# A two-layer attention trunk on one core: new tables of priorities and engine choices for a scheduler that writes the instruction order

## The chip, the cores and the metric

One Trainium2 chip, one of its cores. The metric is the device time of one execution in microseconds (us). A time is a median of several runs; the profile is of one execution.

## The reference

Two layers run over 256 tokens of width 1024. In each, the normalised input `h` goes through one large projection (1024 x 9808); its columns feed three causal attentions of 8 heads, each with a SiLU gate, a projection of its own and a sigmoid merge gate. One more projection adds the result to the residual.

```python
def hybrid_layer(x, gain, w_in, f_bias, w_branch, w_out):
    h = rms_norm(x, gain)
    proj = jnp.einsum('bsd,de->bse', h, w_in)
    (qa, ka, va, ga, qb, kb_, vb_, gb, qc, kc, vc, gc,
     q_idx, k_idx, w_idx, f_logit, merge_logit) = jnp.split(proj, SPLIT_POINTS, axis=-1)
    oa = moba_attention(rope(qa), rope(ka), va) * silu(ga)
    ob = dsa_attention(rope(qb), rope(kb_), vb_, qi, ki, wi) * silu(gb)   # keys chosen by an indexer, top 64
    oc = forgetting_attention(qc, kc, vc, log_f) * silu(gc)
    y = jnp.einsum('nbsw,nwd->bsnd', jnp.stack([oa, ob, oc]), w_branch)
    merged = jnp.sum(sigmoid(merge_logit).reshape(B, S, 3, D_MODEL) * y, axis=2)
    return x + jnp.einsum('bsd,de->bse', merged, w_out)
```

After the two layers stands a last `rms_norm`. All is float32.

## The kernel before

**Matrix products.** Each float32 matrix is split into a high part that TensorE takes in one pass (`wh`, `hTh`, `og0h`) and the remainder (`wl`, `hTl`, `og0l`). A product is three matmuls: high by high, high by remainder, remainder by high. ScalarE (ACT) writes the high part (L444 for weights), VectorE (DVE) the remainder (L448). A weight piece is 128 x 1024 elements; it comes by DMA into one of four `raw` buffers and its parts go into rings of six `wh` and six `wl`.

**Units.** The work is cut into units of one block of outputs each: `unit_b` (128 columns of the input projection by 256 tokens, 24 matmuls), `unit_a` (values and output projection, 512 columns), `unit_m` (merge gates, `mth`), `unit_y` (branch outputs, with L1017 and L1019 merging them). All matmuls of projections are recorded at L486; they write one of three PSUM banks `proj`, and an element-wise instruction must have read a bank before it is used again.

**Attention.** For two heads at a time, `Pair.attend` computes scores, exponentials (L779), the normalised probabilities in two float16 halves (`p hi` at L787 on ScalarE or L790 on VectorE, `p lo` at L794), transposes them by DMA (`t<-e`, L803) and copies the result to float32 (`pt<-t`, L808 on ScalarE or L809 on VectorE). The matmuls L821 to L824 multiply with the values. L837 to L842 apply the gate; GpSimd (POOL) does a few of these products (`og`) and of the merges (`y`).

**Order.** Every operation is an object with a number, a priority `key` (the number of the unit that it belongs to, with an offset) and one or more `ways`: engine, cost in ns, and the function that emits it. Numbers are given in program order and do not depend on the tables below. `Plan.run` is a list scheduler that runs while the program is built: it keeps a clock for each engine from fixed costs, takes the engine that can start first, and among the operations of that engine that could start within a slack of the earliest it emits the one with the lowest key. The slack is 0 for TensorE, 110 ns for ScalarE and VectorE, and 1500 ns for SyncE (SP), which issues nearly all DMAs. What it emits is each engine's static program; at run time the engines wait only for semaphores, each in its own order.

Two tables correct the scheduler:

```python
        o.key += SHIFT.get(o.n, 0.0)
        if len(ways) > 1 and o.n in WAY:
            o.ways = [w + (WAY[o.n],) if w[0] == "DVE" else w for w in ways]
```

A negative `SHIFT` brings an operation forward. A way's extra numbers are added to its end time when ways are compared, so that `WAY` of -1500 forces an operation to VectorE and +1500 forces it away. VectorE's way of a `p hi` or a `pt` copy carries 500 ns (`AWAY`) against it anyway. The scheduler reckons 1250 ns for the issue of a transpose (`T_ISSUE`) and 1500 ns until it has landed (`T_LAND`), always the same, and has no instruction fetches.

The operations that are spoken of by number:

- 0, 1: loads of the first 128 rows of `x`; 3, 4: of the second 128 rows; 71, 80, 89, 98, 116, 125: the weight chunks va0, va1, va2, va3, va5, va6 (256 KB each) that the first units use. Before the shifts, the keys of va0 to va7 are -95 + 0.2 i, those of 3 and 4 -94.7 and -94.69.
- 17, 18, 19: pieces of the first norm; 46: half of the squares of the second 128 rows; 126: the high part of va6.
- 637, 692, 1059, 1391, 2241, 2463: `pt` copies; 548, 909, 2193, 2458: `p hi`, all ten on ScalarE before.
- 2673, 2680: weight loads of `vb` in layer 1; 2754: of `kb`; 3127: the third of the four `w_branch` loads for the last branch of layer 1. Their loads, the transposes and the loads of `w_out` all go through SyncE's queue.
- 3100: matmuls of a unit of that last branch; 3175, 3177, 3212: of the output projection.

Of the kernel before, what the change touches and what calls it, by code (L numbers as in the profile page):

```python
# [63 lines left out]
def constants(forget_bias):  # L64
# [24 lines left out]


SHIFT = {
# [31 lines left out]
}  # L123
WAY = {
# [6 lines left out]
}  # L131


# [1169 lines left out]
```

## Time and profile before

| | us |
|---|---|
| median of 3 runs | 602.27 (600.35 to 602.92) |
| the profiled execution | 601.2 |
| its span, first to last instruction | 599.4 |

The span is what the profile's parts are shares of; 1.8 us of the execution lie around it. A row of a group names line, engine, operation, output and inputs, shapes, count, then busy time and the mean of one in ns. Rows of waits give the waiting instruction, what ended the wait, the total in us, how many, and the longest. Rows of stretches give the bounds, then each engine's busy time and instructions in the order TensorE, its weight loads (PEld), VectorE, ScalarE, GpSimd, then granted clock, DMA share and GB/s. Rows of the timeline and of the chain start with the start and the duration in us. Matmuls overlap: a busy time of 0.28 us of a 128 x 256 matmul is not the distance to the next one.

### The profile page before, as it was taken

The numbers are of one execution on the slowest core, as the hardware profiler recorded it, in microseconds if no ns is written. First come the engines' busy times: TensorE is split into PE (matmuls) and PEld (weight loads), VectorE is DVE, ScalarE is ACT, GpSimd is POOL, SyncE is SP. The second block draws the span as 40 slices with busy tenths as digits, with TensorE's granted clock in tenths as the row PEclk, the third lists the DMA queues.
The fourth block names the chain that finished last, engine by engine and source line by source line (L and its number), as shares of the span: only waits on it lengthen the run. The fifth ranks groups of instructions, "written<-read, shape, count | busy, mean of one in ns | idle before, by whom it ended". The sixth has DMA issues, their size and how long they took to land.

```text
span 599.4 us, 12672 instructions
## 1 busy us (share of the span) xinstructions
PE 587.5 (98%) x4704; PEld 567.8 (95%) x4704; DVE 542.3 (90%) x1360; ACT 463.8 (77%) x1004; POOL 92.4 (15%) x102
## 2 busy tenths in 40 slices
PE   9999999999999999999999999999999999999995
PEld 7999999999998999999889999999999899999885
DVE  8889999989999989999686999999998999999773
ACT  5769669987997879985485874999889787999632
POOL 1042133000000225110000421320000023340000
PEclk9999999999999999999999999999999999999999
DMA  8986286597865866397648447669869486645802
GB/s 314 305 282 210 73 233 182 162 226 213 241 182 140 271 195 164 89 286 245 189 150 262 152 143 235 178 186 208 214 188 256 121 246 208 169 133 129 311 35 72
DMA packets 136510, 116.83 MB, mean 195 GB/s; under 512 B 42752, under 2 KB 127360, under 8 KB 136448
## 3 DMA queue, kind: packets, MB, share of 16 engines
q1 hardware_dynamic: 136160, 115.59, 66.4%
q8 instruction: 37, 0.61, 0.4%
q10 hardware_dynamic: 288, 0.43, 0.2%
q14 instruction: 25, 0.20, 0.1%
HBM read 103.42 MB, written 1.05 MB: 174 GB/s over the span
## 4 chain that ended last, share of the span: by engine, by line
PE 58%; DVE 22%; ACT 9%; DMA 5%; issue 4%; POOL 0%; SPq 0%; POOLq 0%; DVEq 0%; ACTq 0%
PE proj L486 47%; DVE wl L448 7%; PE proj L1173 4%; DMA t<-e 4%; ACT wh L444 2%; PE proj L1113 2%; DVE isc L970 2%; DVE e L794 1%; DVE rsh L535 1%; ACT pt L808 1%; ACT e L779 1%; DVE t L969 1%; DVE isc L949 1%; DMA raw<-in_w_out_dram 1%; DVE rr L537 1%
## 5 line engine op out<-in xcount | busy, mean ns | idle before, releaser
L486 PE MATMUL proj<-hTh,wh 128*128 128x256 f32 x1024 | 265.7, 278 | 1.5 <-ACT mth L986 1.0
L486 PE MATMUL proj<-hTl,wh 128*128 128x256 f32 x1024 | 265.0, 277 | 0.0
L448 DVE TENSOR_TENSOR wl<-raw,wh 128x1024 fp32r<-128x1024 f32 x180 | 223.3, 1249 | 15.2 <-ACT wh L444 14.0
L486 PE MATMUL proj<-hTh,wl 128*128 128x256 f32 x1024 | 227.9, 276 | 0.0
L444 ACT ACTIVATE wh<-raw 128x1024 fp32r<-128x1024 f32 x180 | 188.7, 1054 | 38.6 <-PE proj L486 26.3
L486 PEld LDWEIGHTS proj<-hTh,wh 128*128 128x128 f32 x1024 | 192.2, 188 | 2.3 <-ACT mth L986 1.2
L486 PEld LDWEIGHTS proj<-hTl,wh 128*128 128x128 f32 x1024 | 192.2, 188 | 0.0
L486 PEld LDWEIGHTS proj<-hTh,wl 128*128 128x128 f32 x1024 | 172.9, 188 | 0.0
L536 POOL TENSOR_TENSOR rsh<-rsh,cst 128x256 f32<-128x256 f32 x40 | 32.4, 812 | 351.4 <-DVE rsh L535 323.2
L538 POOL TENSOR_TENSOR rr<-rr,rsh 128x256 f32<-128x256 f32 x40 | 45.6, 1140 | 2.8
L779 ACT ACTIVATE e<-e,st 128x128 f32<-128x128 f32 (+1 forms) x96 | 42.6, 445 | 2.9 <-DVE st L775 2.4
L794 DVE SCALAR_TENSOR_TENSOR e<-e,st 128x128 f16<-128x128 f32 (+1 forms) x96 | 40.1, 424 | 1.1 <-ACT e L787 0.4
L808 ACT ACTIVATE pt<-t 128x384 fp32r<-128x384 f16 x73 | 34.3, 513 | 7.1 <-DMA t<-e 6.8
L486 PE MATMUL proj<-wh,v 128*128 128x512 f32 (+1 forms) x144 | 35.2, 366 | 0.0
L486 PE MATMUL proj<-og0l,wh 128*128 128x256 f32 x128 | 33.8, 277 | 0.0
L486 PE MATMUL proj<-og0h,wh 128*128 128x256 f32 x128 | 32.4, 278 | 1.3 <-DVE mth L1017 1.3
L787 ACT ACTIVATE e<-e,st 128x256 f16<-128x256 f32 (+1 forms) x77 | 31.6, 445 | 2.7 <-DVE st L783 2.3
L486 PEld LDWEIGHTS proj<-wh,v 128*128 128x128 f32 x144 | 25.3, 189 | 4.3
L486 PE MATMUL proj<-og0h,wl 128*128 128x256 f32 x128 | 28.6, 276 | 0.0
L486 PEld LDWEIGHTS proj<-og0h,wh 128*128 128x128 f32 x128 | 24.0, 188 | 1.6 <-DVE mth L1017 1.5
L486 PEld LDWEIGHTS proj<-og0l,wh 128*128 128x128 f32 x128 | 24.0, 188 | 0.0
L486 PEld LDWEIGHTS proj<-og0h,wl 128*128 128x128 f32 x128 | 21.7, 188 | 0.0
(227 smaller groups left out, 1071.0 us busy)
## 6 DMA issues: line engine op xcount, KB each, us to landing
raw<-in_w_in_dram SPq DMA_DIRECT2D x74, 1024.0 KB, 5.5
raw<-in_w_branch_dram SPq DMA_DIRECT2D x24, 512.0 KB, 4.2
raw<-in_w_out_dram SPq DMA_DIRECT2D x8, 1024.0 KB, 8.4
raw<-in_x_dram SPq DMA_DIRECT2D x8, 256.0 KB, 4.9
tmp<-wf SPq DMA_DIRECT2D x16, 128.0 KB, 5.5
t<-e SPq DMA_TRANSPOSE x48, 2.9
raw<-in_w_in_dram SPq DMA_DIRECT2D x2, 320.0 KB, 6.2
x<-in_x_dram SPq DMA_DIRECT2D x2, 256.0 KB, 3.8
```

The costliest lines, as they stand in the source:

```text
L444: ACT.activation(p[0].v, sel(c.v), AF.Copy)
L448: DVE.tensor_tensor(p[1].v, sel(c.v), p[0].v.bitcast(F32), op=ALU.subtract)
L486: PE.matmul(o(), a(), b(), start=first and i == 0, stop=last and i == n - 1)
L536: gps(lambda: POOL.tensor_tensor(T(sh)[:np_], T(sh)[:np_], s[:np_], op=ALU.mult), S, [k_rope], [sh], key, "rope")
L538: gps(lambda: POOL.tensor_tensor(T(r)[:np_], T(r)[:np_], T(sh)[:np_], op=ALU.add), S, [sh], [r], key, "rope")
L779: act(lambda t=t, a=a, n=n, st=st, h=h: ACT.activation(ex(h, a, n), ex(h, a, n), AF.Exp, bias=T(st)[:, t:t + 1], scale=-1.0, accum_out=T(s ...
L787: ACT.activation(hi(a, n), ex(h, a, n), AF.Copy, scale=T(st)[:, 4 + t:5 + t])
L794: dve(lambda t=t, a=a, n=n, st=st, h=h, hi=hi, lo=lo: DVE.scalar_tensor_tensor(lo(a, n), ex(h, a, n), T(st)[:, 4 + t:5 + t], hi(a, n), op0 ...
L808: plan.op([("ACT", t_act(384, False), lambda to=to, src=src: ACT.activation(to(), src(), AF.Copy)), ("DVE", t_dve2(384), lambda to=to, src ...
L970: dve(lambda o=o, t8=t8: DVE.match_replace(o, T(t8), o, TAKEN), n, [t8], [k_isc[i]], key + r * step, "top8")
L1113: PE.matmul(T(ps[t]), h(i, t), v(w, n), start=left[t] == 23, stop=left[t] == 0)
L1173: PE.matmul(T(ps[t])[:, :w], hA[hi](a + x, t), T(p[wi])[:, ats[w > 256][wi]][:, :n * w].rearrange("p (k c) -> p k c", k=n)[:, x], start=le ...
```

## The change

Only the two tables are replaced: `SHIFT` has 315 entries instead of 327, `WAY` 47 instead of 53. 134 numbers have a shift in both (27 of them the same), 193 lose theirs, 181 get one. In `WAY`, 28 entries forced to VectorE and 25 away from it; now 31 and 16. The new values come from a replay of the order outside the kernel that also counts the fetches of instructions by DMA; `Plan.run` itself, its costs and all operations are the same.

```diff
 SHIFT = {
-    0: -11.5, 1: -7, 3: -11.5, 4: -11, 17: 2, 28: -8, 31: -6, 47: -11, 73: 4, 80: -12, 89: -2.5, 90: -11.5, 91: 1.5,
-    98: -8, 99: -9.5, 100: 2.5, 188: 3, 308: -7, 310: -7, 364: 6, 380: 2.5, 386: -12, 387: -7, 419: 3.5, 440: -11,
...
-    2672: 2.5, 2675: -12, 2678: -12, 2680: -4.5, 2688: -6.5, 2697: -12, 2701: -8.5, 2755: -12, 2774: -12, 2780: -3,
...
-    2940: -9.5, 2941: -12, 2942: -12, 2943: -12, 2945: 3.5, 2962: -12, 2964: -8.5, 2969: -9, 2989: -4, 2991: -11,
-    2992: -3, 3009: -4, 3044: -12, 3046: -9, 3048: -8, 3076: -12, 3079: -11.5, 3127: -7, 3175: -12, 3177: 6, 3212: 5,
+    0: -12, 1: -7.5, 3: -12, 4: -10.5, 18: -2.5, 19: -7.5, 22: -4.5, 28: -12, 31: -5.5, 38: -8, 46: -12, 47: -12,
+    55: -12, 71: -11.5, 80: -3.5, 89: -8.5, 90: -3.5, 91: 2, 98: -12, 100: 5, 116: -5.5, 117: -11.5, 125: -4.5,
+    126: -3, 174: -9, 186: -12, 187: 2, 188: 2.5, 218: -8.5, 219: -8, 220: -12, 221: -2.5, 228: 4, 243: -5, 263: 6,
...
+    2641: -11.5, 2652: -7.5, 2653: 6, 2669: -12, 2670: -12, 2673: -7, 2678: -12, 2680: -12, 2754: -12, 2780: -2,
...
+    2962: -11.5, 2973: -3.5, 2980: -12, 2985: -6, 2986: 5.5, 3005: -6, 3009: -9.5, 3018: -12, 3044: -6.5, 3046: -12,
+    3048: -12, 3050: -9.5, 3076: -12, 3100: -12,
 }
 WAY = {
-    17: -1500, 18: -1500, 90: -1500, 99: 1500, 489: 1500, 490: 1500, 539: 1500, 552: -1500, 553: -1500, 559: 1500,
-    631: 1500, 632: -1500, 650: -1500, 675: 1500, 687: -1500, 845: -1500, 862: -1500, 863: -1500, 914: -1500,
-    915: -1500, 996: 1500, 1215: 1500, 1240: 1500, 1283: -1500, 1290: 1500, 1373: -1500, 1391: 1500, 1392: -1500,
-    1416: 1500, 1417: -1500, 1443: 1500, 1489: 1500, 2115: -1500, 2194: 1500, 2207: -1500, 2211: -1500, 2212: -1500,
-    2249: -1500, 2255: 1500, 2411: -1500, 2558: -1500, 2571: -1500, 2603: -1500, 2661: 1500, 2790: 1500, 2791: 1500,
-    2802: 1500, 2827: 1500, 2841: 1500, 2846: -1500, 2852: 1500, 2940: 1500, 3009: -1500,
+    18: 1500, 19: -1500, 46: 1500, 90: -1500, 126: -1500, 509: 1500, 534: -1500, 547: 1500, 548: -1500, 631: 1500,
+    637: -1500, 692: -1500, 845: -1500, 862: -1500, 863: -1500, 909: -1500, 915: -1500, 1059: -1500, 1216: -1500,
+    1283: -1500, 1290: 1500, 1349: -1500, 1373: -1500, 1379: 1500, 1391: -1500, 1392: -1500, 1417: -1500, 1443: 1500,
+    1489: 1500, 2115: -1500, 2193: -1500, 2207: -1500, 2241: -1500, 2249: -1500, 2254: 1500, 2255: 1500, 2458: -1500,
+    2459: -1500, 2463: -1500, 2558: -1500, 2790: 1500, 2827: 1500, 2841: 1500, 2846: -1500, 2852: 1500, 3005: 1500,
+    3009: -1500,
 }
```

50 rows, old and new, of the table SHIFT are left out of this document.

## Prediction

> **What bounds the kernel now.** First the page's busy shares and queue rows, then the stretches, to see whether TensorE is bound by its own work.
>
> ```profile
> span 599.4 us, 12672 instructions
> PE 587.5 (98%) x4704; PEld 567.8 (95%) x4704; DVE 542.3 (90%) x1360; ACT 463.8 (77%) x1004; POOL 92.4 (15%) x102
> PEclk9999999999999999999999999999999999999999
> q8 instruction: 37, 0.61, 0.4%
> q14 instruction: 25, 0.20, 0.1%
> 135.00:150.00 15.00, 15.00 (x133) 14.95 (x132) 14.83 (x29) 11.65 (x20) 0.00 (x0) 1.00 0.70 213
> 105.00:120.00 15.00, 13.98 (x122) 13.68 (x121) 13.91 (x46) 14.76 (x41) 0.00 (x0) 1.00 0.56 160
> ```
>
> TensorE (PE) is busy for 98% of the span at nearly full granted clock. In the full stretch, 135 to 150, it starts 133 matmuls, one per 113 ns; in the stretch from 105 to 120 only 122. Eleven missing matmuls are 1.2 us. A new order changes no matmul, so it can win only such holes. The waits of TensorE list them (two rows of the first 7 us, before the projections begin, are left out).
>
> ```profile
> PE proj L486 <- DVE mth L1017: 1.3, 1, 1.3
> PE o L821 <- ACT pt L808: 1.1, 3, 0.5
> PE proj L486 <- ACT mth L986: 1.0, 1, 1.0
> PE proj L486 <- DVE g L736: 0.3, 2, 0.2
> PE proj L486 <- DVE rr L537: 0.3, 1, 0.3
> ```
>
> These are 4.0 us in 8 waits. A wait costs more than its idle time, because a busy matmul overlaps the next one. The timeline of TensorE at one of them shows how much:
>
> ```profile
> 100.07 0.28 PE L821 MATMUL o<-pt,v 128*128 128x256 f32 x1
> 100.19 0.22 PE L822 MATMUL o<-pt,v 128*128 128x128 f32 x1
> 100.30 0.28 PE L824 MATMUL o<-pt,v 128*64 128x256 f32 x1
> 101.02 0.39 PE L821 MATMUL o<-pt,v 128*128 128x256 f32 x1 [0.44 <-ACT pt L808]
> 101.25 0.22 PE L822 MATMUL o<-pt,v 128*128 128x128 f32 x1
> ```
>
> Undisturbed, the next start comes 0.12 us after a 128x256 matmul (100.07 to 100.19). Across the wait it is 0.72 (100.30 to 101.02): 0.60 lost for 0.44 idle, 0.16 more. The restarted matmul then holds its successor 0.23 instead of 0.12, another 0.11. So each wait costs its idle time plus 0.27, and all eight cost 4.0 + 8 x 0.27 = 6.2 us. That is the most a new order can win; everything below is a share of it.
>
> Which of them hang on a DMA is told by the chain of work and by two more rows of the timeline:
>
> ```profile
> 93.39 4.31 DMA t<-e
> 127.87 5.77 DMA t<-e
> 415.90 6.45 DMA t<-e
> 471.23 4.81 DMA t<-e
> 553.30 7.85 DMA raw<-in_w_out_dram
> DMA to landing us min/median/max: 2.7/2.9/6.7
> 479.53 0.50 PE L486 MATMUL proj<-wh,hTh 128*128 128x512 f32 x1 [0.16 <-DVE g L736]
> 563.87 0.39 PE L486 MATMUL proj<-og0h,wh 128*128 128x256 f32 x1 [1.34 <-DVE mth L1017]
> ```
>
> A transpose of the probabilities (`t<-e`, L803) lands 2.9 us after its issue in the median; the kernel's own scheduler reckons 1.25 + 1.5 = 2.75. The four in the chain took 4.3 to 6.5. Each stands ahead of a hole: 101.02 follows the first; the other two waits for `pt` follow the second and third; the one at 479.53 follows the fourth, through ScalarE and `g`. In an in-order queue a `pt` copy that waits for a late transpose holds everything behind it. These four holes cost 1.1 + 3 x 0.27 = 1.9, and 0.16 + 0.27 = 0.4: together 2.3 us. The wait at 563.87 costs 1.34 + 0.27 = 1.6; it stands behind the load of `w_out`, as VectorE shows:
>
> ```profile
> 559.00 0.42 DVE L477 SCALAR_TENSOR_TENSOR og0l<-ot,og0h 128x256 fp32r<-128x256 f32 x1
> 562.26 1.23 DVE L448 TENSOR_TENSOR wl<-raw,wh 128x1024 fp32r<-128x1024 f32 x1 [2.84 <-ACT wh L444]
> 563.40 0.75 DVE L1017 SCALAR_TENSOR_TENSOR mth<-mth,proj 128x256 f32<-128x256 f32 x2
> ```
>
> VectorE sat 2.84 us before a weight split whose data were late; the release of a `proj` bank (L1017) was queued behind it. The remaining waits (`mth` L986, `rr` L537, the other `g`: 1.0 + 0.3 + 0.2 idle, three waits) cost 2.3 and stand behind other element-wise work, not a DMA.
>
> **The change part by part.** The instructions and their total stay; only order and some engines change.
>
> *Fetches.* The queue rows show 37 + 25 fetches: 0.61 MB / 37 is 16 KB each, and one comes every 599.4 / 37 = 16 us. An order made with them can place `pt` copies and their matmuls later behind a transpose that a fetch meets. Bounds: nothing, and 6.2 (all waits). I take the four late transposes, -2.3: the nearest rows, since all four are late by 1.4 us or more against the median, and a fetch every 16 us can't account for much beyond them. When these holes go, the next things late are the three element-wise waits.
>
> [...]
>
> *Engine choices.* Prices from the rows of each line:
>
> ```profile
> L808 ACT ACTIVATE pt<-t x73: 502/510/528, 97.7 to 552.7; 128x384 fp32r<-128x384 f16 x73
> L809 DVE CAST pt<-t x23: 342/353/902, 114.3 to 554.9; 128x384 fp32r<-128x384 f16 x23
> L787 ACT ACTIVATE e<-e,st x77: 386/404/513, 89.9 to 548.3; 128x128 f16<-128x128 f32 x39, 128x256 f16<-128x256 f32 x38
> L790 DVE TENSOR_SCALAR e<-e,st x19: 268/345/356, 96.1 to 513.5; 128x256 f16<-128x256 f32 x10, 128x128 f16<-128x128 f32 x9
> ```
>
> Six `pt` copies and four `p hi` copies that ran on ScalarE are now forced to VectorE: +6 x 0.353 + 4 x 0.345 = 3.5 us on VectorE, -(6 x 0.510 + 4 x 0.404) = -4.7 on ScalarE. Seven `pt` and four `p hi` lose their force to VectorE: up to 7 x 0.353 + 4 x 0.345 = 3.9 back, if all return to ScalarE. Net on VectorE -0.4 to +3.5 of its 542.3, on ScalarE -4.7 to 7 x 0.510 + 4 x 0.404 - 4.7 = +0.5. One `og` and one `y` product go to GpSimd and four `og` lose their force to it; GpSimd has 507 us idle. I cost all this at 0: it lies beside TensorE's matmuls, and TensorE's banks cover it. Without that cover, in a stretch like 135 to 150 where VectorE has 14.83 of 15, it costs up to 3.5; at best it gains the 2.3 of the element-wise waits.
>
> *Start.* By the keys, the third load is now half of `x` instead of the weight chunk va1, and va0 comes fourth, va3 fifth. The first weights land one load later.
>
> ```profile
> 0.00:15.00 15.00, 13.54 (x63) 11.23 (x64) 12.83 (x40) 8.79 (x22) 2.06 (x8) 1.00 0.89 314
> 5.68 0.69 DVE L1107 TENSOR_TENSOR wl<-raw,wh 128x512 fp32r<-128x512 f32 x1
> 7.42 0.50 PE L1113 MATMUL proj<-wh,hTh 128*128 128x512 f32 x1
> ```
>
> 256 KB at 314 GB/s is 0.8 us. Both halves of the first chunk are ready at 5.68 + 0.69 = 6.37, 1.05 before the first matmul that uses it, so the cover is the norm and its transposes, and the cost 0. If that cover is gone, +0.8; if the earlier `x` helps, -0.8. The norm pieces trade engines (one to ScalarE, one to VectorE, the squares to ScalarE): small against the 0.8 and inside the same bounds.
>
> *Weight loads on SyncE.* Two loads of the `vb` section and one of `kb` in layer 1 move up by 7 to 12 steps of priority, so transposes queued near them may stand behind a load of 1 MB; one late `w_branch` load loses its -7 and is now sorted behind the last transposes. What may move either way is the wait at 563.87. I take 0, with -1.6 (it goes) and +1.6 (the earlier loads double it) as ends.
>
> *Priorities of the rest.* 481 entries differ; in the order of before these operations stand on VectorE (228), ScalarE (132), TensorE (96), SyncE (17) and GpSimd (8). TensorE takes the next ready matmul without slack, so an early one can't idle it. Element-wise reorderings make and remove holes like the three of 2.3 us; I cost them at 0, between -2.3 and +2.3.
>
> The sum is -2.3 us. Its own execution took 601.2 us (span 599.4 and 1.8 around it), 1.1 below the median of the three times, 602.27 (600.35 to 602.92). I set the sum against the middle of the two, 601.7, and forecast **599.4**.
>
> **Rivals.** *All holes go.* For it: the eight holes are short, and an order that knows when DMAs land may avoid all. Against it: three have no DMA behind them, and whatever the plan leaves out returns elsewhere. 601.7 - 6.2 = 595.5.
>
> *The fetches are hidden anyway.* Then the new order is only another one, with holes of its own of about the old size: 601.7. For it: the fetch queues carry 0.4% and 0.1%, and a load of 1 MB ahead of a transpose is a likelier cause of a landing of 6.5 than one packet. Against it: holes do stand behind late transposes.
>
> *Slower: the end of layer 1.* The `w_branch` load that lost its -7 goes behind the last four transposes on SyncE's in-order queue, and the `w_out` loads behind it. Price: up to four issues of the transposes' row.
>
> ```profile
> L803 SPq DMA_TRANSPOSE t<-e x48: 1210/1217/2062, 93.4 to 550.5; - x48
> ```
>
> That is 4 x 1.22 = 4.9 us; TensorE already waits there, so nothing covers it: 601.7 + 4.9 = 606.6. It decides once the slip exceeds the gain, 2.3, by 3. Against it: the loads have a ring of four buffers, and a priority counts only among instructions that are ready at nearly the same time.
>
> **How the numbers follow.** Chances: forecast (one half to one and a half of -2.3) 0.46; all holes 0.20; hidden 0.21; slower 0.13. About 0.5% (3.0 us of 602.27) is what a measurement of this kernel can tell from no change: 599.3 to 605.3. The forecast's middle lies on that edge, so I split it 0.20 faster, 0.26 same; all holes: 0.20 faster; hidden: 0.21 same; slower: 0.10 slower and 0.03 same. Faster 0.40, same 0.50, slower 0.10. The likeliest case's own range is 601.7 less 1.2 to 3.5: 598.2 to 600.5. The range for 8 in 10 reaches to the all-holes case, 595.5, and above the hidden case, 601.7, by the element-wise end, 2.3: 604.0. It leaves out the slower case and a little below.
>
> **What would show it.** TensorE's waits for `pt` and for `g` behind the transposes gone, its total of 4.0 us idle at 2.5 or below: the main step right. `t<-e` of 4 us and more still in the chain, with other work behind them: fetches placed, not removed. A wait for L1017 near 564 of other than 1.3 prices the loads. VectorE's busy time between 542 and 546 shows the engine choices. The prediction is wrong if new waits of TensorE, at places that have none now, add up to more than 1 us, or if matmuls start later than 7.4 us.

## The result, and the profile after

The new kernel takes **598.14 us** (median of 6 runs, 597.86 to 599.87), the old one 602.18 beside it: the ratio is 0.9945, 95% interval 0.9922 to 0.9968. By the ratio it is faster by 0.55%, 3.3 us; the two medians lie 4.0 us apart. 599.4 was forecast. The profiled execution took 597.9 us and its span is 596.1, 3.3 less than before.

Lines of the new kernel's page, its waits of TensorE (the one row before 6 us left out), one stretch, and the landing of the transposes (in the new file each line number is one lower; in the kernels of the experiments it is shifted by a few lines):

```profile
span 596.1 us, 12662 instructions
PE 586.0 (98%) x4704; PEld 567.6 (95%) x4704; DVE 539.3 (90%) x1362; ACT 464.4 (78%) x1003; POOL 92.2 (15%) x101
q8 instruction: 37, 0.61, 0.4%
PE proj L485 <- DVE mth L1016: 1.3, 1, 1.3
PE o L820 <- DVE ot L838: 0.8, 1, 0.8
PE s L608 <- ACT tmp L593: 0.6, 1, 0.6
PE proj L1112 <- ACT hTh L615: 0.6, 1, 0.6
105.00:120.00 15.00, 15.00 (x134) 14.85 (x133) 14.53 (x46) 14.84 (x40) 3.29 (x3) 1.00 0.65 181
DMA to landing us min/median/max: 2.7/3.4/6.8
```

Of the eight waits of before, six are gone; the places at 131 to 134 and at 239 have longer ones. The stretch from 105 to 120, which had 122 matmuls, has 134. But the transposes don't land sooner: their median rose from 2.9 to 3.4 us, and 19 of 48 take over 4 us where 15 did. The new order lives with late transposes; it does not avoid them.

What each hole cost TensorE (distance between matmul starts, less the undisturbed distance of that shape, with the slower matmuls just behind it):

| at (us) | what was waited for | before | after |
|---|---|---|---|
| start | first norm, `hTh` | - | +0.9 |
| 101 | `pt`, late transpose | 0.9 | - |
| 111 | `mth`, element-wise | 1.3 | - |
| 131 to 134 | `pt`, then `ot`, late transpose | 0.6 | 1.1 |
| 239 | `rr`, then `mth` | 0.6 | 1.6 |
| 368, 383 | `g`, score maximum, element-wise | 0.5, 0.4 | - |
| 426, 480 | `pt`, `g`, late transpose | 0.6, 0.4 | - |
| 564 | `mth`, late `w_out` | 1.6 | - |

6.9 us went and 3.6 came, a balance of 3.3 us. That it equals the gain of the span is chance, because the last matmul ends only 2.6 us earlier: about 0.7 us go again in steps too small for this table. The other 0.7 us of the gain lie behind the last matmul, where the span went on for 6.3 us and now goes on for 5.7. The last matmuls and the last store that SyncE issues, old kernel first, then the new:

```profile
592.68 0.40 PE L486 MATMUL proj<-wl,v 128*128 128x256 f32 x2
595.93 0.33 SPq L672 DMA_DIRECT2D out_dram<-tmp  x1
```

```profile
590.04 0.40 PE L485 MATMUL proj<-wl,v 128*128 128x256 f32 x2
592.92 0.38 SPq L671 DMA_DIRECT2D out_dram<-tmp  x1
```

Counted from the end of the last matmul (593.08 and 590.44), the old kernel issues this store 0.4 us later. By the packet records an 8 KB instruction fetch on queue q14 starts 2.2 us before the old kernel's end; the new kernel's last one is 36 us before its end. All the kernels below fall into the same two groups: the two with the old tables and other warm-ups, and `way_only`, have the late fetch and 6.3 us behind the last matmul, the others have neither (5.7 us). The four long ends are those of the kernels with 347 instructions on SyncE, the others have 349 to 352. That the late fetch is one of SyncE's own program, and the cause, is a guess; no run changes that alone.

The new holes in the timeline of TensorE, and the transposes ahead of them in the chain:

```profile
8.42 0.50 PE L1112 MATMUL proj<-wh,hTh 128*128 128x512 f32 x1 [0.60 <-ACT hTh L615]
131.43 0.39 PE L820 MATMUL o<-pt,v 128*128 128x256 f32 x1 [0.79 <-DVE ot L838]
239.41 0.39 PE L485 MATMUL proj<-hTh,wh 128*128 128x256 f32 x1 [1.32 <-DVE mth L1016]
122.72 6.78 DMA t<-e
230.15 5.60 DMA t<-e
```

Both holes inside have the old cause. The `pt` copy waits on ScalarE for its transpose, the half-products `ot` queue behind it, VectorE waits for these, and the release of a bank (`o` at 131, `proj` through `mth` at 239) comes last.

### The profile page after: what moved, and what is told of

Its sections match the earlier page's. It is cut to its first block, busy times and chain, and to the rows that moved or that the text cites. A ratio compares the mean times of both kernels' runs of the same rounds, so it can differ in the third digit from the quotient of the medians.

```text
span 596.1 us, 12662 instructions
## 1 busy us (share of the span) xinstructions
PE 586.0 (98%) x4704; PEld 567.6 (95%) x4704; DVE 539.3 (90%) x1362; ACT 464.4 (78%) x1003; POOL 92.2 (15%) x101
## 3 DMA queue, kind: packets, MB, share of 16 engines
HBM read 103.42 MB, written 1.05 MB: 175 GB/s over the span
## 4 chain that ended last, share of the span: by engine, by line
PE 82%; ACT 7%; DVE 6%; DMA 3%; issue 2%; POOL 1%; SPq 0%; POOLq 0%; DVEq 0%; ACTq 0%
PE proj L485 69%; PE proj L1172 4%; DMA t<-e 2%; PE proj L1112 2%; PE s L708 2%; PE s L706 2%; ACT wh L443 2%; DVE wl L447 1%; PE o L820 1%; PE o L823 1%; ACT e L778 1%; DVE isc L969 1%; ACT pt L807 1%; DMA x<-in_x_dram 1%; ACT e L786 1%
## 5 line engine op out<-in xcount | busy, mean ns | idle before, releaser
L535 POOL TENSOR_TENSOR rsh<-rsh,cst 128x256 f32<-128x256 f32 x40 | 36.3, 908 | 301.1 <-DVE rsh L534 288.8
L537 POOL TENSOR_TENSOR rr<-rr,rsh 128x256 f32<-128x256 f32 x40 | 43.5, 1088 | 3.6 <-ACT qx L692 0.8
L786 ACT ACTIVATE e<-e,st 128x128 f16<-128x128 f32 (+1 forms) x76 | 31.0, 445 | 1.7 <-DVE e L793 0.7
L836 ACT ACTIVATE ot<-o 64x256 f32<-64x256 f32 x48 | 18.2, 380 | 6.5 <-PE o L823 4.3
```

The costliest lines, as they stand in the source:

```text
L535: gps(lambda: POOL.tensor_tensor(T(sh)[:np_], T(sh)[:np_], s[:np_], op=ALU.mult), S, [k_rope], [sh], key, "rope")
L537: gps(lambda: POOL.tensor_tensor(T(r)[:np_], T(r)[:np_], T(sh)[:np_], op=ALU.add), S, [sh], [r], key, "rope")
L786: ACT.activation(hi(a, n), ex(h, a, n), AF.Copy, scale=T(st)[:, 4 + t:5 + t])
L836: act(lambda r=r, h=h: ACT.activation(T(t)[r], T(o)[64:, h * S:(h + 1) * S], AF.Copy), S, True, [o], [kt[h]], key, "og", touch=[t], half=True)
```

## The experiments

Each ran beside the old kernel on the same chip, in three sessions on three chips; ratios are to the old kernel beside it. The first two diffs name the tables in short; the files hold the entries themselves.

### Is the gain made place by place?

The scheduler finishes one layer in the same state with either table, so that tables of both can be joined: on either side of a cut, every engine's order is exactly that of the kernel that the table is from.

```diff
-SHIFT, WAY = new, new
+SHIFT, WAY = (old if n < 1690 else new for each operation n)    # old0_new1
+SHIFT, WAY = (new if n < 1690 else old for each operation n)    # new0_old1
+SHIFT, WAY = (old if n < 150 else new for each operation n)     # old_start
+SHIFT, WAY = (old if n < 150 or 1140 <= n < 1690 else new)      # mix
```

> Layer 0 with the old tables, layer 1 with the new ones (operation numbers below and from 1690); each layer's instructions then stand in exactly the order of the kernel that its tables are from. Theory A, the gain is made place by place: TensorE's five holes of layer 1 before (0.46 at 368, 0.28 at 383, 0.57 at 426, 0.43 at 480, 1.62 at 564; 3.4 us together) go and those of layer 0 before stay: 602.2 - 3.4 = 598.8 us. Theory B, the new order works only as a whole, since every fetch and load meets other work when layer 0 is another: holes come back in layer 1, 600 to 602 us.

Measured: 598.3 us, 0.9955 (0.9939 to 0.9971). The gain against the old kernel beside it, 601.11, is 2.8 us where A has 3.4, and 0.7 of it is the shorter end, which A did not count. Past the first 8 us, TensorE's waits in this kernel's profile are those of the old layer 0 alone (at 101, 111, 135 and 239):

```profile
PE o L819 <- ACT pt L806: 1.2, 2, 0.8
PE proj L484 <- ACT mth L984: 1.0, 1, 1.0
PE proj L484 <- DVE rr L535: 0.3, 1, 0.3
```

> Layer 0 with the new tables, layer 1 with the old ones. Theory A: layer 0 wins its four old holes (0.9 at 101, 1.3 at 111, 0.64 at 134, 0.57 at 239; 3.4 us) and loses as much again in a later start (0.9) and two new holes (1.1 at 131, 1.6 at 239): 602.2 us, no change. Theory B: 600 to 602 us, the gain spread over both layers.

Measured: 599.8 us, 0.9981 (0.9967 to 0.9996): a small gain against A's "no change". It has the shorter end, 0.7 us, and its profile shows a second reason why it is better than A reckoned: the wait at 564, which cost 1.6, is nearly absent (0.3), with the old tables there. The old holes at 368 and 383 stay, with 0.5 and 0.4. (The profiled execution took 601.19 us, 1.4 above the median, so its holes don't add up to the median's gain.)

```profile
564.53 0.39 PE L488 MATMUL proj<-og0h,wh 128*128 128x256 f32 x1
PE proj L488 <- DVE mth L1019: 1.5, 1, 1.5
PE o L823 <- DVE ot L841: 0.9, 1, 0.9
```

So the 1.6 us of that hole are not a lasting property of the old order of layer 1; they come and go with the landing of the first load of `w_out`, which took 7.8 us before, 6.4 here and 6.2 to 6.3 in the two shifted old kernels below (none of these three has the hole). The other two lines are the new layer 0's own holes.

> The new tables, but the old ones for operations below 150 (the loads of x and of the first weights, the first norm, the first weight splits). Theory A: the first matmul of the projections starts near 7.4 us again instead of 8.4, and what follows is as in the new kernel: 598.1 - 0.9 = 597.2 us. Theory C, the start is bound by the landing of the weight chunks whatever the norm does: within 0.3 us of the new kernel, 598.1.

Measured: 597.35 us, 0.9939 (0.9924 to 0.9953). The first matmul of the projections starts at 7.53 instead of 8.42, and the two holes after it stay, the one at 131 with 1.3 us idle instead of 0.8: A by the profile, and by the median (597.2 forecast), though the interval overlaps that of the new kernel. What the new start does wrong is in ScalarE's timeline, new kernel first, then the old:

```profile
6.09 0.63 ACT L558 ACTIVATE acc<-x 128x512 f32<-128x512 f32 x1 [3.87 <-DMA x<-in_x_dram]
6.72 1.00 ACT L593 ACTIVATE tmp<-xg,small 128x128 f32<-128x128 f32 x2
```

```profile
5.74 0.51 ACT L594 ACTIVATE tmp<-xg,small 128x256 f32<-128x256 f32 x1 [3.52 <-POOL small L568]
6.16 0.61 ACT L559 ACTIVATE acc<-x 128x512 f32<-128x512 f32 x1
```

In the new kernel, ScalarE's norm pieces stand behind the squares of the second half of the rows, which wait for a DMA until 6.09; before, the piece came first, at 5.74. This run takes back the engine choices and the order of the loads together; the next section parts them.

> As the run with the old start, and the old tables also for the b branch of layer 0 (operations 1140 to 1689); everything else new. Theory A: the new hole of 1.6 at 239 is replaced by the old one of 0.57 there: 597.2 - 1.0 = 596.2 us. Theory B: another hole of about 1 us opens where the two orders meet: 597 to 598 us.

Measured: 596.9 us, 0.9934 (0.9916 to 0.9953), the lowest time of this study, though its interval overlaps that of the new one; A had 596.2 and B 597 to 598. The hole at 239 is the old one again, as A says, and the one at 131 stays:

```profile
PE o L819 <- DVE ot L837: 1.0, 1, 1.0
PE proj L484 <- DVE rr L535: 0.3, 1, 0.3
```

### Does either table do it alone?

```diff
-SHIFT, WAY = new, new
+SHIFT, WAY = new, old     # shift_only
+SHIFT, WAY = old, new     # way_only
```

> The new priorities with the old engine choices. Theory A (gain by place, each place needing its priorities and its engines together): places whose choices differ lose their fit and new holes open in both layers; 600 to 604 us, no faster than the old kernel. Rival: the priorities carry the gain and the ten copies forced to VectorE are beside the point: 598 to 599 us.

> The new engine choices with the old priorities. Theory A: as above, 600 to 604 us. Rival: the engine choices, which take 4.7 us off ScalarE ahead of late copies, carry the gain: 598 to 599 us.

Measured: the new priorities with the old choices 603.58 us, 1.0036 (1.0021 to 1.0051); the new choices with the old priorities 608.13, 1.0111 (1.0085 to 1.0137). Both rivals fall. The second is also 4 us above the 600 to 604 of theory A: the size of the loss was not foreseen. The longest wait of the latter, and VectorE's timeline ahead of it:

```profile
PE proj L487 <- DVE g L737: 3.7, 3, 3.1
251.39 0.17 DVE L783 RECIPROCAL st<-st 128x2 f32<-128x2 f32 x1 [0.76 <-ACT e L780]
251.92 0.41 DVE L737 SCALAR_TENSOR_TENSOR g<-th,proj 128x256 f32<-128x256 f32 x1
```

One `g` product, 0.41 us long, holds TensorE for 3.1 us: it stands in VectorE's queue behind softmax work that itself waits for ScalarE. Choices and priorities are one plan.

The two runs also part the new start. First the new priorities, and so the new order of loads, with the old choices; then the new choices with the old loads:

```profile
7.83 0.51 PE L1112 MATMUL proj<-wh,hTh 128*128 128x512 f32 x1 [0.75 <-DVE wl L1106]
```

```profile
8.61 0.47 PE L1114 MATMUL proj<-wh,hTh 128*128 128x512 f32 x1
```

The loads alone move the first matmul from 7.42 to 7.83, where it waits for the remainder `wl` of the first chunk; that chunk lands at 6.6 instead of 5.2. The choices alone move it to 8.61. The two do not add up: both together give 8.42.

### Is the new order fitted to the moments of the fetches?

TensorE has 2 x 4704 instructions (matmuls and weight loads) and queue q8 37 blocks: one fetch for 254 instructions. By the packet records of the old kernel, neighbouring fetches start 255.6 TensorE instructions (200 to 312) and 15.8 us apart in the mean. More warm-up matmuls at the start move the fetches against the work (the q8 packet that started at 112.3 us in the old kernel started at 105.5 with 88 of them); they were meant to change nothing else:

```diff
-    for _ in range(WARM):
-        PE.matmul(warm[:, :128], ones, ones, start=True, stop=True)
+    w16 = ones.bitcast(mybir.dt.bfloat16)[:, :128]
+    for _ in range(88):            # 64 in the runs "third"
+        PE.matmul(warm[:, :128], w16, w16, start=True, stop=True)
```

> The new tables; the 12 float32 warm-up matmuls at the start (24 passes) are 88 bfloat16 ones, which fill about the same time but put 128 more instructions ahead on TensorE. A fetch block of TensorE is 256 instructions, so each of its fetches then meets the work half a block, about 7 us, earlier. Theory F, the new order gains because it is fitted to the moments of the fetches: some transposes that were met by none are late now and the order has left no room for them; 599 to 601 us. Theory G, late landings come from the loads queued ahead and the fetches hardly matter: within 0.7 us of 598.1, the holes at 131 (1.0) and 239 (1.5) stay, and the transpose issued near 230.2 still lands after about 5.6 us.

> The old tables with the same 88 warm-up matmuls. Theory F: the holes behind transposes that a fetch of TensorE met (0.9 at 101, 0.43 at 480) shrink or go, others may open elsewhere; the set of holes is another one, the time 600 to 603 us. Theory G: the same holes at the same places (101, 111, 134, 239, 368, 426, 480, 564), within 0.7 us of the old kernel.

Measured: new 598.69 us, 0.9960 (0.9943 to 0.9977); old 600.61, 0.9988 (0.9976 to 1.0001). By time alone both lie within the 0.7 us of theory G. But both sets of holes changed, as F says. The 88 matmuls took 7.2 us in the old kernel instead of 5.3 (the 12 float32 ones are 24 records in the trace), so it also starts 1.4 us later (8.84); with that taken off, an estimate, it would be at 0.9965 and about even with the new order, which starts at 8.56 here instead of 8.42. In the new order the hole at 131 went, the one at 239 stayed with 0.8 us idle, and a new one of 1.7 us opened at 403, behind a transpose that landed after 7.1 us:

```profile
PE s L708 <- ACT bd1h L863: 1.7, 1, 1.7
392.73 7.12 DMA t<-e
```

In the old order, the holes behind late transposes and the one at 564 went and the element-wise ones stayed:

```profile
PE proj L487 <- ACT mth L987: 1.4, 1, 1.4
PE proj L487 <- DVE rr L538: 0.3, 1, 0.3
PE proj L487 <- DVE g L737: 0.2, 1, 0.2
```

The pair of runs also gives the price of a fetch by itself: the same transpose, at the same place in the program, with a fetch and without. First the transpose ahead of the hole at 480 and its twin in the half-period run, then one of the new kernel without a fetch and its twin that a fetch meets:

```profile
L803 SPq DMA_TRANSPOSE t<-e x1: 1217/1217/1217, 471.2 to 471.2; - x1
DMA to landing us min/median/max: 4.8/4.8/4.8
```

```profile
L804 SPq DMA_TRANSPOSE t<-e x1: 1212/1212/1212, 472.0 to 472.0; - x1
DMA to landing us min/median/max: 3.4/3.4/3.4
```

```profile
L802 SPq DMA_TRANSPOSE t<-e x1: 1217/1217/1217, 513.9 to 513.9; - x1
DMA to landing us min/median/max: 2.8/2.8/2.8
```

```profile
L802 SPq DMA_TRANSPOSE t<-e x1: 1224/1224/1224, 515.5 to 515.5; - x1
DMA to landing us min/median/max: 4.1/4.1/4.1
```

The fetch starts 1.9 us after the issue of the late one in the first pair, 1.2 in the second, by the packet records. Call a transpose met when a fetch starts 0.3 to 2.6 us after its issue. In 25 pairs of the two orders one twin is met and the other, not met, lands within 3.4 us: the met one lands 1.1 us later in the mean (0 to 1.9). In the 40 such pairs of which neither is met, the shifted twin differs by 0.1 in the mean. The kernels with 64 warm-up matmuls give 0.8 over 22 pairs, against 0.0 over 42.

But a fetch is not the main cause of the latest landings. The transpose issued at 98.9, met by none, takes 4.8 and its twin 4.9; the one at 127.9, 5.8 and 5.0, with no fetch in either; the one ahead of the new hole at 239 takes 5.6 with a fetch 3.5 us after its issue and 5.1 without one. Something else delays these by 2 us and more; the loads queued ahead are the likely cause, which no run here isolates.

> The new tables with 64 bfloat16 warm-up matmuls, which end as early as the 12 float32 ones did and put 80 more instructions ahead on TensorE: its fetches meet the work a third of a block, 4.5 us, earlier. Theory F, each order's holes belong to one placing of the fetches: the new order loses what it was fitted to and comes to about 1.4 us more, 599 to 600 us. Rival H, the new order is the better one at any placing: within 0.5 us of the new kernel on the same chip.

> The old tables with the same 64 warm-up matmuls, so without the later start that the 88 caused. Theory F: the old order loses the holes that its fetches made (at 101, 426, 480, 564), others open at random; some 2 us faster than the old kernel, 599 to 601 us, and within 1 us of the new order at this placing. Rival H: within 0.7 us of the old kernel, 601 to 602 us.

> The new kernel as it is, for its time on the same chip as the two before: 598 us, 3 to 3.5 us below the old one.

> The mix of both orders (old start and old b branch of layer 0, the rest new) with the 64 warm-up matmuls. Theory F: its gain over the new kernel is of the same kind, fitted to one placing; it gives back 1 to 2 us, 598 to 599 us. Rival H: 596.9 us again.

The kernel of new_again is the new one unchanged; mix_third is the mix with the 64 warm-up matmuls.

Measured: new_third 597.77 us, 0.9942 (0.9924 to 0.9960); old_third 600.90, 0.9990 (0.9978 to 1.0001); new_again 598.12, 0.9949 (0.9932 to 0.9965); mix_third 597.58, 0.9933 (0.9917 to 0.9950). Theory F falls here: at this placing, the new order and the mix lose nothing and the old order gains nothing that can be told from no change; by these ratios the new order leads by 0.5%, as at its own placing. Of that lead of 3 us, 0.7 is the shorter end, and another 0.7 is gained by its start, which is earlier here than in the new kernel (7.73). H holds, though not at half a block. In the old order, the element-wise waits are there again, and a late transpose at 135:

```profile
PE proj L487 <- ACT mth L987: 1.4, 1, 1.4
PE proj L487 <- DVE rr L538: 0.9, 1, 0.9
PE o L822 <- ACT pt L809: 0.6, 1, 0.6
```

The profile of new_again warns of reading one execution too closely: the same program had a span of 598.2 instead of 596.1, with three waits for `ot` where there was one.

```profile
PE o L820 <- DVE ot L838: 2.0, 3, 1.0
```

## Why the prediction was right, and where not

The time came out 0.1 us below the likeliest case's own range (598.14; 598.2 to 600.5), well inside the whole one, and the bound of 6.2 us was not passed, although the holes of before measure 6.9: the list of waits has no row for the one at 383, and the cost of the one at 101 was set 0.2 too low. That the number is near is in part luck: the term that was to make the gain gave almost nothing, and terms set at 0 made it. Of the prediction's own signs, the waits for `pt` and `g` went, as it asked. But the start (8.42, later than its 7.4) and VectorE's busy time (539.3, outside 542 to 546) came out wrong, TensorE's idle total (2.7, counted as before) missed its 2.5, and late transposes still in the chain with other work behind them mean "fetches placed, not removed".

- *What bounds the kernel*: right for the most part. 2.6 of the 3.3 us lie in TensorE's run of matmuls, and a join of tables moves the time roughly by the holes of its places. The step missed that 0.7 us could be won behind the last matmul.
- *The four late transposes, -2.3*: their holes went, 2.5 us by the table. What the step missed is that nearly as many were made: 1.1 at 131 and 1.0 more at 239 stand behind other late transposes. Net -0.4, not -2.3. Transposes became later on the whole, not earlier. Nor were all four late through a fetch: a fetch met the ones at 93.4 and 471.2, which take 2.9 and 3.4 without it, and none met the ones at 127.9 and 415.9.
- *Element-wise order, 0 between -2.3 and +2.3*: this is the term that was mis-sized. The holes at 111, 368 and 383 cost 2.2 us and went. They belong to the old order: the wait at 111 is in every old layer 0 that was profiled whole (1.0, 1.0, 1.4 and 1.4 us), at every placing of the fetches, the holes at 368 and 383 in every old layer 1 (0.5 and 0.4 each time), and none of them in a new one. The prediction took such holes to be made as often as removed; the new tables removed them and, at their own placing, made none of that kind. (The lasting new hole, at 239, stands behind a late transpose.)
- *Weight loads, 0 between -1.6 and +1.6*: the low end, 564 gone. By new0_old1 and the shifted old runs this hole goes without any change to layer 1, so it isn't the loads' order that is shown to have removed it.
- *Start, 0 between -0.8 and +0.8*: measured +0.9. The loads cost part of it: the first chunk was ready 1.5 us later (7.91 instead of 6.37), more than its cover of 1.05, and alone that costs 0.4. The larger part is the engine choices of the norm, which were called small: in the new kernel one wait for a DMA came to stand ahead of ScalarE's first piece.
- *Engine choices, 0*: right for ScalarE (464.4 us instead of 463.8) and for the copies, of which as many went back as were forced over, but for one of each kind. VectorE was expected to gain up to 3.5 us of work or to lose 0.4; it lost 3.0. The cost was not 0 at the start. That the choices need their own priorities is shown by the two halves, +0.4% and +1.1%.
- *Rival "hidden"*: half refuted. A fetch costs a transpose that it meets about 1 us, so the cause named for the change is real. But the new order's lead is not bound to the placing of the fetches that it was made for: it is 0.5% there and at a third of a block. Nor is it the same at all: at half a block it is 0.3%, 0.1% of it the shorter end, and about nil with the old kernel's late start taken off. How much of it a replay without fetches would have found is open: none of its plans was here to run.
- *Rivals "all holes" and "slower at the end of layer 1"*: neither came; the end of layer 1 has no wait of TensorE at all.

TensorE itself keeps its pace while a block is fetched: 133 matmuls start from 135 to 150 in the old kernel, with a fetch at 141.4 by the packet records, and 134 from 105 to 120 in the new one, with a fetch at 111.8. A fetch packet of 16 KB takes 1.1 us in the median of its 37 records, about as long as the transposes that it meets are late; whether they wait for its end, no run shows.

## What to carry to other kernels

In a static plan for a nearly full engine, add up that engine's holes first, place by place: they bound what a new order can win there, and tables of two plans can be joined at points where the scheduler's state is the same, to keep the better of each place. Ask of each hole whether it is in every execution (an order to mend) or comes and goes with a landing (then leave room behind the wait rather than chase it). Engine choices and priorities of one plan are not to be mixed with those of another within a place. And look behind the last matmul as well: a fifth of this gain lay there.

## What was not expected of the hardware

A transpose that a 16 KB instruction fetch meets lands 0.8 to 1.1 us later in the means of 22 and 25 pairs, 30 to 40% of the 2.7 of the quickest, although TensorE's fetches together fill 0.4% of the DMA engines' time. A kernel's end is 0.7 us longer in all four kernels with an 8 KB fetch 2.2 us before it than in the ten without. And two executions of one program, in two sessions, differ by 2 us in TensorE's holes (spans of 596.1 and 598.2), well over half of the 3.3 that this change brings: one profile of each kernel would not have told the lasting holes from the passing ones.
